# Attention outputs of both halves in one pool, and two of the second half's read-backs beside the last attention steps

## The chip, the cores and the metric

The kernel runs on one core of one Trainium2 chip. The metric is the device time of one execution in microseconds. Before the change the median of three runs is 1555.2 us (1551.68 to 1557.26). A separate, profiled execution gave the trace that is read here.

The engines are named as in the profile: PE (matrix products; PEld its weight loads), DVE (vector), ACT (scalar), POOL (GpSimd) and SP, which here only issues transfers. PE, DVE, ACT, POOL and SP each run their own list of instructions in order. Matrix products accumulate in PSUM; other tiles lie in SBUF, and "DRAM" names hold data that goes out to the chip's main memory and comes back.

## The reference

One layer of a streaming encoder on x of 1024 positions by 1024 channels, float32. Two attention branches (8 heads of 64 each) share one input projection; each is projected to 1024 channels, both are merged by sigmoid gates, and an output projection, a residual LayerNorm and a gated feed-forward part follow:

```python
proj = h @ w_in[l]
q_a, k_a, v_a, f_a, q_c, k_c, v_c, gate_a, gate_c = jnp.split(proj, split_points, axis=-1)
o_a = _forgetting_attention(heads_a(q_a), heads_a(k_a), heads_a(v_a), f_a + b_f[l])
o_c = _chunk_band_attention(heads_c(q_c), heads_c(k_c), heads_c(v_c), rel_bias[l])
merged = (jax.nn.sigmoid(gate_a) * (o_a @ w_br_fox[l])
          + jax.nn.sigmoid(gate_c) * (o_c @ w_br_chunk[l]))
mix = merged @ w_out[l]
x = _layer_norm(alpha * x + (1.0 + g1) * mix, ln1_g[l], ln1_b[l])
h = _layer_norm(x) * (1.0 + sc2) + sh2
u = _causal_depthwise_conv(h @ w_up[l], conv_w[l], conv_b[l])
a, val = jnp.split(u, 2, axis=-1)
y = (jax.nn.silu(a) * val) @ w_down[l]
x = _layer_norm(alpha * x + (1.0 + g2) * y, ln2_g[l], ln2_b[l])
```

## The kernel before, in words

**Precision.** A float32 product is made of three products of a rounded type: each operand is split into "hi" (a cast) and "lo" (what the cast left). Hence names in pairs: oh and ol, wh and wl, mh and ml; and each product comes as three matmuls, L192 to L194.

**Attention.** It works out unnormalised outputs, head by head, transposed, for two halves of 512 positions. They go to DRAM as od[half, i], 128 rows (two heads) by 512 positions each, i = 0 to 7. i = 4 to 7 is one branch, 0 to 3 the other. The reciprocals of the softmax sums go to rd, one row a head. Between attention steps PE is given pieces of other products (a "stream" of units); the last of these are the gates' pre-activations psg, whose sigmoid's core (ACT, L385) is stored to gd. Preparation of later weights (dr, td) runs on POOL up to about 648 us.

**Read-backs.** An attention output is used as a pair of i: ost<-od (512 KB), two transfers ort<-rd (256 KB each) that broadcast the reciprocals to the partitions of their head, a product (L794), the cast to oh on ACT (L797) and the subtraction to ol on DVE (L798). load_o, a generator, does one pair at each next(). For half 0 it goes through the pairs 4, 6, 2, 0: the first three are issued and multiplied on POOL, while the last attention steps run; the pair 0 is issued on SP and multiplied on DVE. For half 1 it goes through 4, 6, 2, 0, all on SP and DVE, one after each of the merge's first four branches. The transfers land in wop's tags wh and wl, two buffers each, so the third pair needs the buffers of the first.

**Merge.** branch(c, b, half) is a block of 128 channels c, a branch b and a half: 12 matmuls psb (L192 to L194), with branch weights brd and the four oh/ol of the half that belong to b (i = 4 to 7 for b = 1, 0 to 3 for b = 0). The accumulators come from mxp, 6 buffers. DVE multiplies psb with the gate sgl (L932), a tile of 512 KB loaded from gd for each (c, half); after b = 0 it adds the two (L935) and splits the result into m (ACT L940, DVE L941). The order is (0,1,0), (0,0,0), (1,1,0), (1,0,0), (0,1,1), (1,1,1), (0,0,1), (1,0,1), then c = 2 to 7, half by half. SP's list holds the weights, the gates and the read-backs one behind the other. The order within an engine is set by the program's text: an instruction stands where the code issues it, and buffers are given by pools in turn, which wait for the buffer's last reader.

**After it.** mixed is the output projection with w_out pieces (wod), residual and norms, then the up-projection's first heads. ready() loads and splits the first up-weights (sgl<-in_w_up on POOL).

**Pools.** o (half 0's outputs) and m1p are opened at the attention's end, o1 (half 1's) in the merge; after the merge o and o1 are closed, and w2 (w_out pieces 5 to 7) and mx (x rows, norm vectors, x2) are opened in their place.

Of the kernel before, what the change touches and what calls it, by code (L numbers as in the profile page):

```python
# [12 lines left out]
F32 = mybir.dt.float32  # L13
F32R = mybir.dt.float32r
AF = mybir.ActivationFunctionType
ALU = mybir.AluOpType
# [3 lines left out]
P = 128  # L20
S = 1024
D = 1024
NT = S // P
KD = D // P
H = 512
# [3 lines left out]
DH = 64  # L29
# [15 lines left out]
def body(ctx, tc, a, out):  # L45
# [38 lines left out]
    od = dram.tile([2, 8, P, H], F32, name="od", tag="od")  # L84
# [111 lines left out]
    def halves(half):  # L196
        return slice(half * H, (half + 1) * H)
# [583 lines left out]
    sy.dma_start(out=g1row, in_=rowd[0].partition_broadcast(P))  # L781
    m1_cm, m1p = opened(name="m1p", bufs=1, side="right")
    o_cm, op_ = opened(name="o", bufs=1, side="right")

    def load_o(half, os_, pairs, pool, tag, bufs, rpool, rtag, op_, early=0):
        for n, i in enumerate(pairs):
            dma, eng = (po, po) if n < early else (sy, ve)
            st = pool.tile([P, 2, H], F32, name=nm("ost"), tag=tag, bufs=bufs)
            dma.dma_start(out=st, in_=od[half, i : i + 2].rearrange("b p s -> p b s"))
            rt = rpool.tile([P, 2, H], F32, name=nm("ort"), tag=rtag, bufs=bufs)  # L790
            for h in range(2):
                row = rd.rearrange("(p h) s -> h p s", h=2)[h, i : i + 2, halves(half)]
                dma.dma_start(out=rt[h * DH : (h + 1) * DH], in_=row.partition_broadcast(DH))
            eng.tensor_tensor(out=st, in0=st, in1=rt, op=ALU.mult)  # L794
            hi = op_.tile([P, 2, H], F32R, name=nm("oh"), tag=f"oh{i}")
            lo = op_.tile([P, 2, H], F32R, name=nm("ol"), tag=f"ol{i}")
            se.copy(out=hi, in_=st)  # L797
            ve.tensor_sub(out=lo, in0=st, in1=hi)  # L798
            for b in range(2):
                os_[i + b] = (hi[:, b, :], lo[:, b, :])  # L800
# [103 lines left out]
    if True:  # L904
# [10 lines left out]

        def merge(os_, reading):
            ms = [[None] * KD for _ in range(2)]
# [129 lines left out]
        o1_cm.__exit__(None, None, None)  # L1047
        o_cm.__exit__(None, None, None)
# [3 lines left out]
        mx_cm, mx = opened(name="mx", bufs=1)  # L1052
        h_11, h_21 = [], []
# [3 lines left out]
        def rows(n):  # L1057
            for t in range(len(xs), n):
                xs.append(mx.tile([P, D], F32, name=nm("xr"), tag="xr", bufs=4))
                sy.dma_start(out=xs[t], in_=a["x"][t * P : (t + 1) * P, :])  # L1060

        rows(2)
        l1g = mx.tile([P, D], F32, name="l1g", tag="l1g", bufs=1)
        l1b = mx.tile([P, D], F32, name="l1b", tag="l1b", bufs=1)
        sy.dma_start(out=l1g, in_=a["ln1_g"].partition_broadcast(P))
# [4 lines left out]
        def begin(t):  # L1070
            x2s.append((mx if t < 4 else mxb).tile([P, D], F32, name=nm("x2"), tag="x2", bufs=4))
            for g in live:
                next(g, None)
            g = norms(t, xs[t], x2s[t], t < NT - 1)
            next(g)
            for old in live:
                next(old, None)
            live[:] = [g]

        turning = None  # L1080
        for group in ((0, 1), (2,), (3,), (4,), (5,), (6,), (7,)):
# [26 lines left out]

    mx_cm.__exit__(None, None, None)
    wo_cm.__exit__(None, None, None)  # L1110
    hd_cm.__exit__(None, None, None)
    w2_cm.__exit__(None, None, None)
    m1_cm.__exit__(None, None, None)
    x1 = x2s[4:]
    yp_cm, yp = opened(name="yp", bufs=3, side="right")
# [376 lines left out]
```

## Time and profile before

| | |
|---|---|
| median of three runs | 1555.2 us (1551.68 to 1557.26) |
| profiled execution | 1550.4 us, its span 1548.6 us |
| PE busy | 1500.3 us, 97% of the span, 7663 matmuls |
| DVE, ACT, POOL busy | 67%, 47%, 43% |
| DMA | 300.76 MB, 194 GB/s in the mean |
| last attention product | begins at 691.14 us |
| merge's first branch / first branch with c = 2 | 703.96 / 742.37 us |

Times within the span are microseconds from its start. A row of a time line has the start, the duration, the engine and line, the operation with its output and inputs, and in brackets how long the engine had been idle and what released it. An engine name with q (SPq, POOLq) is its issuing of transfers. In the chain of waits, a DMA row lasts from issue to landing. A matmul's own duration (0.39 us) is longer than its spacing, since matmuls are pipelined: the spacing of starts is what counts.

### The profile page before, as it was taken

What the parts mean: (1) busy time and instruction counts of PE and PEld (TensorE: products, weight loads), DVE (VectorE), ACT (ScalarE), POOL (GpSimd) and SP (SyncE); (2) the same over time, 40 slices, a digit from 0 to 9 for tenths busy, and PEclk for the clock granted to TensorE, in tenths of its full rate; (3) what the DMA queues carried; (4) which work ended last, traced back from release to release, by engine and by line L of the source; (5) the groups of instructions that cost most, each with busy time, mean ns of one, the idle gap of its engine ahead of it and who ended that gap; (6) DMA issues with size and microseconds to landing.
All of it is one profiled execution on the core that took longest, in us unless ns stands there. A gap on an engine that the chain in (4) does not pass through costs nothing.

```text
span 1548.6 us, 21684 instructions
## 1 busy us (share of the span) xinstructions
PE 1500.3 (97%) x7663; PEld 1264.7 (82%) x7663; DVE 1031.5 (67%) x2024; ACT 725.5 (47%) x1344; POOL 658.6 (43%) x607
## 2 busy tenths in 40 slices
PE   6999999999999999996999998999999999999996
PEld 3788898889888988885888887888888888888885
DVE  6756666566656565555446786777778776845798
ACT  3555555455444454442113565544544554555451
POOL 0039888887877877630000005454455453000000
PEclk9999999999999999998999999999999999999999
DMA  9157666766666579768764385443344323697552
GB/s 370 47 167 216 213 199 213 218 190 200 215 230 211 182 266 303 246 181 253 244 225 174 129 272 172 136 152 133 123 139 147 116 102 101 240 342 249 191 189 76
DMA packets 121053, 300.76 MB, mean 194 GB/s; under 512 B 12512, under 2 KB 21424, under 8 KB 120944
## 3 DMA queue, kind: packets, MB, share of 16 engines
q1 hardware_dynamic: 81504, 181.05, 35.4%
q0 software_dynamic: 25344, 92.02, 18.0%
q10 hardware_dynamic: 14096, 26.31, 4.8%
q8 instruction: 60, 0.98, 0.3%
q14 instruction: 49, 0.40, 0.1%
HBM read 206.69 MB, written 84.25 MB: 188 GB/s over the span
## 4 chain that ended last, share of the span: by engine, by line
PE 74%; POOL 9%; DMA 8%; DVE 5%; issue 2%; ACT 1%; SPq 0%; DVEq 0%; ACTq 0%; POOLq 0%
PE psu L861 24%; PE psd L1309 4%; PE psd L1310 4%; PE psd L1308 4%; PE pso L508 3%; PE psg L192 3%; PE psg L194 3%; PE psg L193 3%; DMA wod<-dr 3%; POOL dr L553 2%; PE pst L494 2%; POOL acc L559 2%; POOL dr L556 2%; DMA brd<-dr 2%; PE psm L957 2%
## 5 line engine op out<-in xcount | busy, mean ns | idle before, releaser
L861 PE MATMUL psu<-hc,wx 128*128 128x512 f32 x792 | 185.8, 389 | 2.4 <-ACT wx L849 2.0
L861 PEld LDWEIGHTS psu<-hc,wx 128*128 128x128 f32 x792 | 148.5, 188 | 34.0 <-ACT wx L849 2.7
L1157 DVE SCALAR_TENSOR_TENSOR pcv<-u,convp,pcv 128x1024 f32<-128x1024 f32 x88 | 113.2, 1286 | 45.4 <-ACT pcv L1155 44.4
L1298 DVE TENSOR_TENSOR op<-rw,op 128x512 fp32r<-128x512 f32 x146 | 93.3, 689 | 52.9 <-ACT op L1297 52.7
L1297 ACT CAST op<-rw 128x512 fp32r<-128x512 f32 x146 | 85.1, 623 | 87.0 <-PE psd L1310 41.7
L457 ACT ACTIVATE s<-s,mx 128x640 f32<-128x640 f32 (+7 forms) x128 | 94.7, 740 | 54.9 <-DVE mx L451 53.4
L1309 PE MATMUL psd<-op,op 128*128 128x512 f32 x292 | 113.6, 389 | 0.9 <-DVE op L1298 0.9
L1310 PE MATMUL psd<-op,op 128*128 128x512 f32 x292 | 113.6, 389 | 0.0
L1308 PE MATMUL psd<-op,op 128*128 128x512 f32 x292 | 113.1, 389 | 0.0
L497 ACT CAST pt<-pst 128x512 fp32r<-128x512 f32 (+1 forms) x192 | 82.2, 451 | 63.1 <-PE pst L494 61.7
L498 DVE TENSOR_TENSOR pt<-pst,pt 128x512 fp32r<-128x512 f32 (+1 forms) x192 | 96.1, 519 | 17.4 <-ACT pt L497 15.5
L192 PE MATMUL psq<-h1h,wh 128*128 128x512 f32 x256 | 103.8, 407 | 1.7 <-DVE h1h L188 1.3
L192 PE MATMUL psg<-h1h,wh 128*128 128x512 f32 x256 | 103.7, 405 | 0.0
L194 PE MATMUL psq<-h1h,wl 128*128 128x512 f32 x256 | 100.9, 394 | 0.9 <-DVE wl L112 0.9
L193 PE MATMUL psq<-h1l,wh 128*128 128x512 f32 x256 | 100.7, 393 | 0.0
L194 PE MATMUL psg<-h1h,wl 128*128 128x512 f32 x256 | 100.3, 392 | 0.0
L193 PE MATMUL psg<-h1l,wh 128*128 128x512 f32 x256 | 100.2, 391 | 0.0
L556 POOL TENSOR_SCALAR dr<-dr,cond 128x512 f32<-128x512 f32 x56 | 90.9, 1625 | 8.3 <-DMA dr<-in_w_ada 7.3
L508 PE MATMUL pso<-pt,vs 128*128 128x256 f32 x608 | 90.4, 288 | 0.8 <-DVE pt L498 0.8
L508 PEld LDWEIGHTS pso<-pt,vs 128*128 128x128 f32 x608 | 81.3, 191 | 7.9 <-ACT pt L497 3.0
L112 DVE TENSOR_TENSOR wl<-ws,wh 128x1024 fp32r<-128x1024 f32 x38 | 61.1, 1609 | 39.1 <-ACT wh L111 39.1
L494 PE MATMUL pst<-ident,s 128*128 128x128 f32 x528 | 83.1, 273 | 0.8 <-DVE pt L498 0.7
(299 smaller groups left out, 3926.8 us busy)
## 6 DMA issues: line engine op xcount, KB each, us to landing
ws<-in_w_up SPq DMA_DIRECT2D x34, 512.0 KB, 3.8
dr<-in_w_ada POOLq DMA_DIRECT2D x32, 512.0 KB, 4.5
dr<-in_w_down POOLq DMA_DIRECT2D x22, 512.0 KB, 5.1
td<-dr POOLq DMA_DIRECT2D x22, 512.0 KB, 4.8
rw<-td SPq DMA_DIRECT2D x44, 256.0 KB, 4.5
yd<-y SPq DMA_DIRECT2D x20, 512.0 KB, 2.8
rw<-yd SPq DMA_DIRECT2D x40, 256.0 KB, 4.7
rw<-sd SPq DMA_DIRECT2D x33, 256.0 KB, 4.8
```

Of the source, the lines that this page charges most:

```text
L192: pe.matmul(ps, wh, xh, start=start, stop=False)
L193: pe.matmul(ps, wh, xl, start=False, stop=False)
L194: pe.matmul(ps, wl, xh, start=False, stop=stop)
L494: pe.transpose(ps[:, b * P : (b + 1) * P], st[:, c0 : c0 + P], ident)
L498: ve.tensor_sub(out=dl, in0=src, in1=dh)
L508: pe.matmul(ps[:, 0:256], vs[:, h % 2, j0 + j, :], pt[j // 4][:, c, j % 4, :], start=j == 0 and c == 0, stop=j == nj - 1 and c == 1)
L556: po.tensor_scalar_mul(x[:, k % 2, :] if k else acc, x[:, k % 2, :], cond[:, k : k + 1])
L861: pe.matmul(ps, w[:, a_, k, :], h[k][b_], start=first, stop=k == 3 and a_ == 1, skip_group_check=on)
L1157: ve.scalar_tensor_tensor(out=ps, in0=u[b][:, 2 - d : S + 2 - d], scalar=cp[:, 2 - d : 3 - d], in1=ps, op0=ALU.mult, op1=ALU.add)
L1308: pe.matmul(ps[t], g[:, 0, ts], d[:, 0], start=start, stop=False, skip_group_check=on)
L1309: pe.matmul(ps[t], g[:, 0, ts], d[:, 1], start=False, stop=False, skip_group_check=on)
L1310: pe.matmul(ps[t], g[:, 1, ts], d[:, 0], start=False, stop=stop, skip_group_check=on)
```

## The change

Both halves' outputs get one pool o of 16 tiles, opened at the attention's end; m1p is opened later, where o1 was. load_o becomes read_o, a generator with two steps (issue the transfers; multiply and split). Five pairs are read on POOL beside the last attention steps: those of half 0 as before, in tiles of the qs and m1 tags, and the pairs 4 and 6 of half 1 in tiles of the attention's v values (tag vs), one wide tile of which holds a pair's outputs and its reciprocals. The pair 0 of half 0 stays with SP and DVE. The last two pairs of half 1 are issued on SP ahead of the merge's gate loads, into the two buffers of wop, and multiplied after the second and the fourth branch. After the merge, the pool o isn't closed: its tiles are used again, by tag, for the w_out pieces 5 to 7, the x rows, the norm vectors and the first four x2. ready() takes its load buffer from the pool hd.

```diff
-    def load_o(half, os_, pairs, pool, tag, bufs, rpool, rtag, op_, early=0):
...
-            yield
-
-    o0, o1 = {}, {}
-    reading = load_o(0, o0, (4, 6, 2, 0), ap0, "qs", 4, ap0, "m1", op_, 3)
-    for _ in range(3):
-        next(reading)
+    def read_o(half, i, st, rt, early=False):
+        dma, eng = (po, po) if early else (sy, ve)
+        dma.dma_start(out=st, in_=od[half, i : i + 2].rearrange("b p s -> p b s"))
+        for h in range(2):
+            row = rd.rearrange("(p h) s -> h p s", h=2)[h, i : i + 2, halves(half)]
+            dma.dma_start(out=rt[h * DH : (h + 1) * DH], in_=row.partition_broadcast(DH))
+        yield
+        eng.tensor_tensor(out=st, in0=st, in1=rt, op=ALU.mult)
+        hi = op_.tile([P, 2, H], F32R, name=nm("oh"), tag=f"oh{half}{i}")
+        lo = op_.tile([P, 2, H], F32R, name=nm("ol"), tag=f"ol{half}{i}")
+        se.copy(out=hi, in_=st)
+        ve.tensor_sub(out=lo, in0=st, in1=hi)
+        for b in range(2):
+            os_[half][i + b] = (hi[:, b, :], lo[:, b, :])
+        yield
+
+    def wide_of():
+        x = ap0.tile([P, 2, NT, P], F32, name=nm("ost"), tag="vs", bufs=3)
+        return [x[:, j].rearrange("p (b a) c -> p b (a c)", b=2) for j in range(2)]
+
+    os_ = {}, {}
+    reading = []
+    for half, i in ((0, 4), (0, 6), (1, 4), (1, 6), (0, 2)):
+        reading.append(read_o(half, i, *(wide_of() if half else pair_of(ap0, ("qs", "m1"), 4)), True))
+        next(reading[-1])
+    for r in reading:
+        next(r)
     stream.finish(len(stream.units))
     begun()
-    next(reading)
+    for _ in read_o(0, 0, *pair_of(ap0, ("qs", "m1"), 4)):
+        pass
...
-    o1_cm, o1p = opened(name="o1", bufs=1, side="right")
+    m1_cm, m1p = opened(name="m1p", bufs=1, side="right")
...
                 branch(*unit)
-                if n < 4:
-                    next(reading)
+                if n in (1, 3):
+                    for _ in reading.pop(0):
+                        pass
...
-        ms = merge((o0, o1), load_o(1, o1, (4, 6, 2, 0), wop, "wh", 2, wop, "wl", o1p))
+        reading = [read_o(1, i, *pair_of(wop, ("wh", "wl"), 2)) for i in (2, 0)]
+        for r in reading:
+            next(r)
+        ms = merge(reading)
...
-        w2_cm, w2p = opened(name="w2", bufs=3, side="right")
-        ws += [parted_w(wod[k], w2p) for k in range(5, KD)]
+        for tags in (("oh04", "ol04"), ("oh06", "ol06"), ("oh02", "ol02")):
+            ws.append([again(tag, True) for tag in tags])
+            for x, j in zip(ws[-1], (2, 0)):
+                sy.dma_start(out=x.bitcast(F32), in_=wod[len(ws) - 1, j : j + 2].rearrange("j p n -> p j n"))
...
-                    ready(c, hdp, mx)
+                    ready(c, hdp, hdp)
```

POOL's list at the attention's end, before: the last preparation steps (dr, td), then three pairs of half 0 (4, 6, 2), then the first up-weights.

```order
L588 TENSOR_TENSOR dr_6658<-dr_6658 128x512
L595 DMA td<-dr_6658 128x2x512
L789 DMA ost_7787<-od 128x2x512
L793 DMA ort_7789<-rd 64x2x512 x2
L794 TENSOR_TENSOR ost_7787<-ost_7787,ort_7789 128x1024
L793 DMA ort_7799<-rd 64x2x512 x2
L793 DMA ort_7809<-rd 64x2x512
L789 DMA ost_7797<-od 128x2x512
L793 DMA ort_7809<-rd 64x2x512
L794 TENSOR_TENSOR ost_7797<-ost_7797,ort_7799 128x1024
L789 DMA ost_7807<-od 128x2x512
L794 TENSOR_TENSOR ost_7807<-ost_7807,ort_7809 128x1024
```

And now, from the second product on (the first, of the pair 4 of half 1, stands ahead of these; its load from od stands before the last dr step). ost_7784 is half 0's pair 4, ost_7789 its pair 6, ost_7798 half 1's pair 6, ost_7802 half 0's pair 2.

```order
L786 DMA ost_7784<-od 128x2x512
L789 DMA ost_7785<-rd 64x2x512 x2
L791 TENSOR_TENSOR ost_7784<-ost_7784,ost_7785 128x1024
L789 DMA ost_7790<-rd 64x2x512 x2
L789 DMA ost_7803<-rd 64x2x512
L786 DMA ost_7789<-od 128x2x512
L789 DMA ost_7803<-rd 64x2x512
L791 TENSOR_TENSOR ost_7789<-ost_7789,ost_7790 128x1024
L786 DMA ost_7798<-od 128x2x512
L789 DMA ost_7798<-rd 64x2x512 x2
L791 TENSOR_TENSOR ost_7798<-ost_7798 128x1024
L786 DMA ost_7802<-od 128x2x512
```

Three products in a row have become five, and two pairs of half 1 have come among those of half 0; the reciprocals of half 0's pair 2 are still asked for early.

SP's list at the merge's start, before and then now (wh and wl from brd are branch weights, sgl the gates; the first pair after them is half 1's 4 before, and its 2 now):

```order
L913 DMA wh_7969<-brd 128x2x512
L913 DMA wl_7970<-brd 128x2x512
L926 DMA sgl_7914<-gd 128x2x512
L789 DMA ost_7930<-od 128x2x512
L793 DMA ort_7932<-rd 64x2x512 x2
L789 DMA ost_7959<-od 128x2x512
L793 DMA ort_7961<-rd 64x2x512 x2
L926 DMA sgl_7973<-gd 128x2x512
L789 DMA ost_7989<-od 128x2x512
L793 DMA ort_7991<-rd 64x2x512 x2
```

```order
L921 DMA wh_7979<-brd 128x2x512
L921 DMA wl_7980<-brd 128x2x512
L786 DMA ost_7925<-od 128x2x512
L789 DMA ost_7926<-rd 64x2x512 x2
L786 DMA ost_7927<-od 128x2x512
L789 DMA ost_7928<-rd 64x2x512 x2
L934 DMA sgl_7939<-gd 128x2x512
L934 DMA sgl_7983<-gd 128x2x512
```

Four pairs have become two, and the first gate load has moved behind them.

DVE's list there now (before, an L932 pair and its sum stood ahead of the first product of half 1):

```order
L795 TENSOR_TENSOR ol_7829<-ost_7802,oh_7828 128x1024
L795 TENSOR_TENSOR ol_7895<-ost_7888,oh_7894 128x1024
L791 TENSOR_TENSOR ost_7925<-ost_7925,ost_7926 128x1024
L795 TENSOR_TENSOR ol_7976<-ost_7925,oh_7975 128x1024
L791 TENSOR_TENSOR ost_7927<-ost_7927,ost_7928 128x1024
L940 SCALAR_TENSOR_TENSOR sgl_7939<-sgl_7939,psb_7941 128x512
L940 SCALAR_TENSOR_TENSOR sgl_7939<-sgl_7939,psb_7955 128x512
L795 TENSOR_TENSOR ol_8020<-ost_7927,oh_8019 128x1024
L943 TENSOR_TENSOR sgl_7939<-sgl_7939 128x512
```

The two products of half 1 that are left (ost_7925 its pair 2, ost_7927 its pair 0) now stand ahead of the first gate products L940 (L932 before), and the subtraction of the pair 0 behind two of these.

More of the change, by code (lines that the diff above doesn't have):

```diff
@@ L781, in body @@
     sy.dma_start(out=g1row, in_=rowd[0].partition_broadcast(P))
-    m1_cm, m1p = opened(name="m1p", bufs=1, side="right")
     o_cm, op_ = opened(name="o", bufs=1, side="right")
-    def load_o(half, os_, pairs, pool, tag, bufs, rpool, rtag, op_, early=0):
[L786 to L800, printed above, removed]
-            yield
@@ new lines, in pair_of @@
+    def pair_of(pool, tags, bufs):
+        return [pool.tile([P, 2, H], F32, name=nm("ost"), tag=t, bufs=bufs) for t in tags]
+    def wide_of():
[6 more added lines that the diff above has]
+        next(reading[-1])
@@ L914, in parted_w, with merge @@
             return parts
-        def merge(os_, reading):
+        def merge(reading):
             ms = [[None] * KD for _ in range(2)]
@@ L1058, in rows @@
             for t in range(len(xs), n):
-                xs.append(mx.tile([P, D], F32, name=nm("xr"), tag="xr", bufs=4))
+                xs.append(again(("oh00", "ol00", "oh14", "ol14")[t % 4]))
                 sy.dma_start(out=xs[t], in_=a["x"][t * P : (t + 1) * P, :])
         rows(2)
-        l1g = mx.tile([P, D], F32, name="l1g", tag="l1g", bufs=1)
-        l1b = mx.tile([P, D], F32, name="l1b", tag="l1b", bufs=1)
+        l1g, l1b = again("oh16"), again("ol16")
         sy.dma_start(out=l1g, in_=a["ln1_g"].partition_broadcast(P))
@@ L1070, in begin @@
         def begin(t):
-            x2s.append((mx if t < 4 else mxb).tile([P, D], F32, name=nm("x2"), tag="x2", bufs=4))
+            x2s.append(again(("oh12", "ol12", "oh10", "ol10")[t]) if t < 4 else
+                       mxb.tile([P, D], F32, name=nm("x2"), tag="x2", bufs=4))
             for g in live:
@@ L1107, in body @@
             head(c)
-    mx_cm.__exit__(None, None, None)
     wo_cm.__exit__(None, None, None)
     hd_cm.__exit__(None, None, None)
-    w2_cm.__exit__(None, None, None)
     m1_cm.__exit__(None, None, None)
+    o_cm.__exit__(None, None, None)
     x1 = x2s[4:]
```

5 lines of the change are left out of this document (2 added, 3 removed).

## The prediction

> **What bounds the kernel now.** I read the page first, then a table of windows over the end of the attention and the merge, then who TensorE (PE) waits for, then the chain of waits through the stage, then the time lines of the engines and queues in it.
>
> The page, and the windows of the stages:
>
> ```profile
> span 1548.6 us, 21684 instructions
> PE 1500.3 (97%) x7663; PEld 1264.7 (82%) x7663; DVE 1031.5 (67%) x2024; ACT 725.5 (47%) x1344; POOL 658.6 (43%) x607
> ```
>
> ```profile
> 680.00:690.00 10.00, 10.00 (x61) 8.50 (x61) 5.81 (x10) 3.87 (x8) 0.21 (x1) 1.00 0.44 145
> 690.00:703.00 13.00, 13.00 (x66) 11.10 (x65) 5.59 (x6) 5.35 (x7) 0.00 (x0) 1.00 0.54 190
> 703.00:742.00 39.00, 27.37 (x100) 20.55 (x100) 17.47 (x20) 6.51 (x8) 0.00 (x0) 0.82 0.86 254
> 742.00:790.00 48.00, 48.00 (x214) 39.74 (x213) 24.76 (x37) 5.74 (x10) 0.00 (x0) 1.00 0.73 246
> ```
>
> The columns are the window, its length, the busy time (instructions) of PE, PEld, DVE, ACT and POOL, the granted clock, the DMA engines' share and GB/s. PE is the bound nearly everywhere; one stretch stands out. From 703 to 742 it is busy 27.37 of 39 us, at a clock of 0.82, while DMA is at 0.86. Before and after it PE is full. Of the 48.3 us that PE idles in the whole span, this stretch holds 11.6. POOL does nothing from 690 to 790, and DMA is half idle from 680 to 703. Who PE waits for, from 690 to 810:
>
> ```profile
> PE psb L192 <- ACT oh L797: 10.7, 2, 7.4
> PE psb L193 <- DVE ol L798: 0.9, 2, 0.5
> ```
>
> So all of it is the merge's first matmuls waiting for the attention outputs of the second half, "hi" (cast on ACT, L797) and "lo" (subtracted on DVE, L798). PE's time line, and then the chain of waits, there:
>
> ```profile
> 703.96 0.39 PE L192 MATMUL psb<-oh,wh 128*128 128x512 f32 x1
> 714.61 0.39 PE L194 MATMUL psb<-oh,wl 128*128 128x512 f32 x1
> 718.33 0.77 PE L192 MATMUL psb<-oh,wh 128*128 128x512 f32 x2 [3.33 <-ACT oh L797]
> 719.59 0.79 PE L193 MATMUL psb<-ol,wh 128*128 128x512 f32 x1 [0.49 <-DVE ol L798]
> 724.25 0.50 PE L193 MATMUL psb<-ol,wh 128*128 128x512 f32 x1 [0.39 <-DVE ol L798]
> 734.20 1.22 PE L192 MATMUL psb<-oh,wh 128*128 128x512 f32 x2 [7.38 <-ACT oh L797]
> 742.37 0.39 PE L192 MATMUL psb<-oh,ws 128*128 128x512 f32 x1
> ```
>
> ```profile
> 704.16 0.61 ACT sg L385
> 704.79 5.70 DMA gd<-sg
> 710.50 0.57 SPq L793
> 711.24 10.34 DMA sgl<-gd
> 721.76 1.28 DVE sgl L932 x2
> 723.04 1.16 DVE ol L798
> ...
> 725.33 6.39 DMA ort<-rd
> ...
> 733.11 1.05 ACT oh L797
> ...
> 736.26 0.43 PE psb L194
> ```
>
> The four branches of half 0 run without a wait from 703.96 to 714.61: 47 steps in 10.65 us, 0.2266 us a matmul. The first eight branches have 96 matmuls, 21.75 us at that pace. They took 742.37 - 703.96 = 38.41, so **16.66 us are lost**: 3.33 + 0.49 + 0.39 + 7.38 = 11.59 in waits, and 5.07 in slow matmuls after them (0.43 each at 736.26). The four pairs of half 1 are loaded through two buffers, so the third pair's product must wait until the first pair is split, and its load starts only then.
>
> **The change, part by part.** I write half/pair.
>
> *Two read-backs go from SP and DVE, in the merge, to POOL, before it.* The rows that price POOL's steps, and the queues that meet them:
>
> ```profile
> 648.47 0.73 POOL L789 DMA_DIRECT2D ost<-od  x1
> 657.52 3.09 POOL L794 TENSOR_TENSOR ost<-ost,ort 128x1024 f32<-128x1024 f32 x1 [6.16 <-DMA ort<-rd]
> 660.92 1.82 POOL L793 DMA_DIRECT2D ort<-rd  x3 [0.31 <-POOL ost L794]
> 670.11 2.39 POOL L794 TENSOR_TENSOR ost<-ost,ort 128x1024 f32<-128x1024 f32 x1 [6.00 <-DMA ost<-od]
> 672.43 0.75 POOL L789 DMA_DIRECT2D ost<-od  x1
> 676.87 3.34 POOL L794 TENSOR_TENSOR ost<-ost,ort 128x1024 f32<-128x1024 f32 x1 [3.69 <-DMA ost<-od]
> ...
> 682.98 1.31 SPq L793 DMA_DIRECT2D ort<-rd  x2
> ...
> 691.14 1.12 PE L508 MATMUL pso<-pt,vs 128*128 128x256 f32 x8
> ```
>
> A step costs POOL 12.1 us (648.47 to 660.61), 11.6 (660.92 to 672.50), and 7.8 where its reciprocal rows were asked for a step early (672.43 to 680.21). Now there are five, in the order 1/4, 0/4, 0/6, 1/6, 0/2, the first begun about a microsecond sooner because its first load stands ahead of two of POOL's last stores. By these rows they end at about 660, 671, 683, 695 and 702; with the later loads in the stretch where DMA is only 0.44 to 0.54 busy, I take **701** for the fifth. What waits for it: ACT's casts stand in order, the fifth ahead of the last two gate activations. The last of these ran at 704.16, and ahead of it the fifth cast (1.05), another activation (0.61) and the cast of 0/0 (1.05) must fit, so the fifth product may end at 701.4 without cost. Beyond that, each microsecond delays the gates' store by one. The cover is thin but there.
>
> The third product meets SP: the reciprocal load of 0/0 was issued at 682.98 and reuses a buffer that POOL's third product now frees, at about 683. DVE's product of 0/0 stands ahead of the last probability splits, on which PE's last eight value matmuls at 691.14 hang. Cost by the rows: nothing; about a microsecond later it would reach PE one for one.
>
> The Trainium skill, "SBUF — State Buffer", section "Who interferes with whom", says that a DVE instruction with two SBUF inputs contends with a GpSimd instruction that reads SBUF. By it, two more POOL products could hold DVE up for as long as they last, at most 2 x 3.34 = 6.7 us, and the forecast would lose what of that reached PE. The trace agrees that POOL's products vary from 2.39 to 3.34 us, but shows no PE wait beside the three that it has, so I put nothing into the sum for it.
>
> *What PE then runs without a wait.* The first six branches use 0/all and 1/4, 1/6 only: 72 x 0.2266 = 16.3 us, from 703.96 to **720.3**. The waits of 3.33, 0.49 and 0.39 go. The last two branches, (0,0,1) and (1,0,1), need 1/0.
>
> *The two read-backs that stay* (1/2, 1/0) are issued ahead of the gate loads:
>
> ```profile
> 704.90 0.41 SPq L926 DMA_DIRECT2D sgl<-gd  x1
> 708.26 2.82 SPq L793 DMA_DIRECT2D ort<-rd  x2
> 711.97 1.29 DVE L932 SCALAR_TENSOR_TENSOR sgl<-sgl,psb 128x512 f32<-128x512 f32 x2 [10.24 <-DMA sgl<-gd]
> 715.98 1.22 DVE L794 TENSOR_TENSOR ost<-ost,ort 128x1024 f32<-128x1024 f32 x1 [0.61 <-DMA ort<-rd]
> 720.62 1.23 DVE L794 TENSOR_TENSOR ost<-ost,ort 128x1024 f32<-128x1024 f32 x1 [1.08 <-DMA ort<-rd]
> ```
>
> Before, the first two pairs on SP landed at 715.98 and 720.62, with one gate load (512 KB) ahead; the second pair's last piece could not be issued until 710.50, when the gates' store had landed. Now that gate load is gone, a first up-weight load of 512 KB comes in on POOL's queue instead, and the last piece waits for branch weights only. I take 0.9 us off: the product of 1/0 at 719.7.
>
> *The gate loads slip.* SP's first now stands behind these and waits for the last gates' store, which landed at 710.49. It lands 7.1 us (704.90 to 711.97) to 10.3 us (the second one, 711.24 on) after issue: 717.6 to 720.8. With two pairs and the branch weights ahead of it, as that second one had, I take 720.8. PE has six accumulators for branches, so the seventh branch needs the first freed by DVE's L932, which needs that gate. DVE's order is product of 1/0, two L932, then the lo of 1/0, just as it was at 720.62, 721.76 and 723.04; then PE's third matmul came at 724.25. 0.9 us earlier: **723.3**.
>
> *The end of the first eight branches.* Two matmuls of the seventh run ahead; 22 x 0.2266 = 5.0 more give 728.3. PE idles some 2.5 us at 720.3. Will the clock fall? Windows of 2 us:
>
> ```profile
> 716.00:718.00 2.00, 0.00 (x0) 0.00 (x0) 1.20 (x1) 0.77 (x1) 0.00 (x0) 1.00 1.07 247
> 718.00:720.00 2.00, 1.17 (x3) 0.70 (x4) 1.23 (x1) 0.28 (x1) 0.00 (x0) 0.72 1.05 246
> 720.00:722.00 2.00, 2.00 (x6) 1.52 (x6) 1.38 (x2) 0.12 (x1) 0.00 (x0) 0.50 0.74 232
> ```
>
> After the gap of 3.33 us the clock was 0.72 and 0.50 for 4 us: 0.28 x 2 + 0.50 x 2 = 1.6 us lost. After 0.39 us nothing is seen. 2.5 is nearer to 3.33, so I charge 1.6: **729.9**, where it was 742.37. The Trainium skill, "TensorE: Matmul & The Clock Gate", section "What's actually happening", says the clock falls after an idle window of about 3.4 us. By it the shorter gap would cost no clock; the trace's 3.33 us gap lies at its edge and did cost it. By the rule the sum would be 1.6 us better.
>
> *The rest.* The wider pool takes over the buffers of later w_out pieces, x rows and norm vectors; their loads keep their places and the releases they wait for come no later, and PE is full from 742 to 790. DMA has room: over 703 to 790 it worked 39 x 0.86 + 48 x 0.73 = 69 of 87 us, and less of that work is left for 74.5. I charge 0.
>
> **Sum**: 742.4 - 729.9 = **12.5 us** less. The profiled execution, 1550.4 us around a span of 1548.6, becomes 1537.9. It lies 4.8 us under the median of the runs shown; on the median's scale 1555.2 - 12.5 = **1542.7 us**.
>
> **The rivals.**
>
> *A. POOL's queue is a little late, or the loads in the merge are.* POOL's fifth product at 703.2 (all steps at 11.6 and 7.8, no help from the quieter DMA) puts the gates' store, the gate load and the seventh branch 1.8 us back; DMA at 1.05 to 1.07 in the merge may hold the gates to 723 as well. Gain 8 to 11: 1544 to 1547. For it: little slack at 701.4. Against: landing is the larger part of a step (6.00 and 6.16 us of idle), and should be shorter where DMA is half idle.
>
> *B. The loads come sooner.* The gate at 717.6 and 1/0 with it: hardly a stall, no lost clock. Gain up to 16.6: 1538.6. Against it: DMA at 1.05 to 1.07 from 716 to 720, so nothing lands faster.
>
> *C. POOL's third product is really late (the loss).* If a step takes much longer with more loads at once, the load of 0/0 waits for it on SP, DVE stands with that product ahead of the last probability splits, and PE stops at 691 with everything behind. Price one for one beyond 684; the gain is eaten when the third product ends at about 696.5 instead of 683, three steps of 16 us, and beyond that the kernel is slower: at 18 us a step, by some 5 us, 1560. For it: two pairs more share POOL and the DMA engines there. Against: no step so far took over 12.1.
>
> *D. The merge starts its later branches earlier, and waits for weights or gates there instead.* The branches of c = 2 and 3 run 12 us sooner, on loads that SP issues behind the same queue. Against: those 69 us of DMA work, less two pairs (1 MB each, 4 us at 254 GB/s), still fit into 74.5; the gain is lost only if the loads keep their old times. Time: 1553 to 1556.
>
> **How the numbers follow.** Forecast 0.5, A 0.25, B 0.08, C 0.07 (0.05 of it a loss), D 0.1. The forecast's own range is 1541 to 1545. Timed runs of this kernel differ by 5.6 us, so I allow 2 us below B and for a part of D above A: 1537 to 1552. 0.3%, 4.7 us, is about what a measurement of this kernel can tell from no change. Faster by more: forecast, A, B and a small part of C and D, 0.86; same 0.08; slower 0.06.
>
> **What would show it.** Right: POOL's five products from 656 to 701; no PE wait up to 720; one wait of 2 to 3 us at the seventh branch, on ACT's cast or DVE's lo of 1/0 or L932; the first matmul with c = 2 near 730; the end of the merge 12 us sooner and the span with it. Wrong: waits at 691 (C), at 707 to 715, several microseconds at 720 (A), waits between 730 and 800 (D), or equal stage times with gaps downstream.

## The result, and the profile after

The changed kernel takes 1546.82 us in the median of 12 runs (1540.68 to 1549.31), the kernel before 1553.85 (12 runs, 1550.63 to 1562.56). The ratio is **0.995, interval 0.9932 to 0.9968**: about 7.0 us faster by the medians, clear of the 0.3% that was taken for no change, and some way short of the 12.5 forecast. In two later sets, beside other runs of the kernel before, the ratio was 0.992 (0.9895 to 0.9945) and 0.9946 (0.9927 to 0.9965), by the medians some 9.4 and 9.0 us.

The first trace of the changed kernel is of its fastest run, 1540.7 us around a span of 1538.9. Its windows of the stages, with the columns as before:

```profile
680.00:690.00 10.00, 10.00 (x57) 8.29 (x57) 5.97 (x13) 4.25 (x9) 4.29 (x4) 1.00 0.93 296
690.00:703.00 13.00, 11.76 (x64) 9.88 (x63) 4.90 (x5) 5.13 (x8) 5.48 (x3) 1.00 0.80 258
703.00:742.00 39.00, 37.47 (x163) 30.18 (x162) 24.38 (x31) 8.97 (x12) 0.59 (x1) 1.00 0.83 281
742.00:790.00 48.00, 48.00 (x213) 39.77 (x212) 23.21 (x35) 5.59 (x9) 0.00 (x0) 1.00 0.65 221
```

From 703 to 742 PE is now busy 37.47 of 39 us at full clock, where it had 27.37 at 0.82. But something new stands ahead of it: from 690 to 703 PE has lost 1.24 us, and from 680 to 690 the DMA engines are 0.93 busy, where they were 0.44. Who PE waits for, from 640 to 810:

```profile
PE pso L508 <- DVE pt L498: 1.2, 1, 1.2
PE psb L194 <- DMA wl<-brd: 1.2, 1, 1.2
PE psb L193 <- DVE ol L795: 0.3, 1, 0.3
```

The two long waits for the second half's outputs are gone, and only 0.3 us of waiting for it is left. The two waits of 1.2 us are new: for the last probability splits of the attention (L498), and for branch weights. PE's time line:

```profile
696.08 2.06 PE L508 MATMUL pso<-pt,vs 128*128 128x256 f32 x15 [1.24 <-DVE pt L498]
...
716.26 0.50 PE L194 MATMUL psb<-oh,wl 128*128 128x512 f32 x1 [1.18 <-DMA wl<-brd]
...
727.80 0.50 PE L193 MATMUL psb<-ol,wh 128*128 128x512 f32 x1 [0.35 <-DVE ol L795]
...
732.95 0.39 PE L192 MATMUL psb<-oh,ws 128*128 128x512 f32 x1
```

The first branch with c = 2 begins at 732.95, not 742.37. The merge's first branch, though, began at 708.89 (before: 703.96). So the first eight branches took 24.1 us instead of 38.4, 14.3 less, and 4.9 us were lost before them.

**How much of that is chance.** The same gate activation (ACT, L385), in a part of the program that the change doesn't touch, starts in the two traces at

```profile
580.30 0.60 ACT L385 ACTIVATE sg<-psg 128x512 f32<-128x512 f32 x1 [1.39 <-PE psg L194]
```

```profile
582.38 0.60 ACT L385 ACTIVATE sg<-psg 128x512 f32<-128x512 f32 x1 [2.32 <-PE psg L194]
```

The first row is of the kernel before, the second of the changed one: 2.1 of the 4.9 us were there before anything had changed. In all 14 traces of this study the activation lies between 578.4 and 583.5. The times from it on are therefore what is compared below: from it to the merge's first branch (A), from there to the merge's last matmul (M), and from that to the end of the span (R), worked out from the rows of each trace in the same way.

| trace | A | M | R |
|---|---|---|---|
| before | 123.7 | 103.5 | 741.2 |
| changed, first trace | 126.5 | 89.1 | 740.9 |
| changed, second (e1) | 133.9 | 90.0 | 740.9 |
| changed, third (e11) | 129.3 | 91.5 | 741.4 |

M is 12.0 to 14.4 us shorter, and R is the same within 0.3. What differs from run to run is A: 2.8, 10.2 and 5.6 us longer than before. Means: M 13.3 us gained, A 6.2 lost, 7.1 left. The timed medians differ by 7.0, 9.4 and 9.0 us in the three sets; means of three traces against a single one of before can't be held to more than that.

### The profile page after: what moved, and what is told of

Its sections match the earlier page's. It is cut to its first block, busy times and chain, and to the rows that moved or that the text cites. A ratio compares the mean times of both kernels' runs of the same rounds, so it can differ in the third digit from the quotient of the medians.

```text
span 1538.9 us, 21695 instructions
## 1 busy us (share of the span) xinstructions
PE 1499.2 (97%) x7663; PEld 1263.4 (82%) x7663; DVE 1032.2 (67%) x2022; ACT 723.9 (47%) x1344; POOL 665.0 (43%) x615
## 4 chain that ended last, share of the span: by engine, by line
PE 85%; DVE 6%; DMA 4%; POOL 2%; issue 1%; ACT 1%; DVEq 0%; ACTq 0%; POOLq 0%; SPq 0%
PE psu L869 25%; PE pso L508 4%; PE psd L1323 4%; PE psd L1324 4%; PE psd L1322 4%; PE psg L192 3%; PE psg L193 3%; PE psg L194 3%; PE pst L494 3%; PE psq L194 3%; PE psq L193 3%; PE psq L192 3%; PE psv L295 2%; PE psv L294 2%; PE psv L296 2%; PE pss L442 2%
## 5 line engine op out<-in xcount | busy, mean ns | idle before, releaser
L498 DVE TENSOR_TENSOR pt<-pst,pt 128x512 fp32r<-128x512 f32 (+1 forms) x192 | 96.0, 518 | 17.7 <-ACT pt L497 15.9
L112 DVE TENSOR_TENSOR wl<-ws,wh 128x1024 fp32r<-128x1024 f32 x38 | 63.5, 1671 | 39.2 <-ACT wh L111 39.2
```

The lines of the kernel that those rows point to most:

```text
L498: ve.tensor_sub(out=dl, in0=src, in1=dh)
```

## The experiments

The question was then what makes the attention's end late, and by so different amounts. Theory A: the two added read-backs crowd it. Rivals: the pool, the added products, or chance. M, A and R of all the kernels are in the table at the end of this section.

**e1, the changed kernel again.**

> The changed kernel once more, for a second trace. In the first trace the merge's first branch began at 709.1 us (before: 704.0) and the branches with c = 0 and 1 took 23.9 us (before: 38.4). Theory A (the two added read-backs crowd the transfers at the attention's end, and the merge starts about 3 us late for it, the other 2 us being chance): merge start 706 to 710. Rival C (all 5 us were chance): merge start 703 to 706. Where the timed runs of the changed kernel lie 6 us above the first trace, something of 3 to 6 us must show here that the first trace did not have, a lower clock after a wait being the candidate. Ratio 0.995.

Median of the timed runs 1544.3 us; the traced run took 1549.6. The merge began at 716.8, later than any theory had it. SP's and DVE's time lines and, last, POOL's, in this trace:

```profile
687.76 0.32 SPq L470 DMA_DIRECT2D rd<-rt  x1
694.20 1.31 SPq L789 DMA_DIRECT2D ost<-rd  x2
...
681.41 3.05 DVE L112 TENSOR_TENSOR wl<-ws,wh 128x1024 fp32r<-128x1024 f32 x1
...
686.78 0.95 DVE L469 RECIPROCAL rt<-psr 32x128 f32<-32x128 f32 x1 [1.65 <-PE psr L464]
...
699.63 1.23 DVE L791 TENSOR_TENSOR ost<-ost,ost 128x1024 f32<-128x1024 f32 x1 [7.23 <-issue]
700.77 1.28 DVE L498 TENSOR_TENSOR pt<-pst,pt 128x512 fp32r<-128x512 f32 x2
...
680.99 2.39 POOL L791 TENSOR_TENSOR ost<-ost,ost 128x1024 f32<-128x1024 f32 x1 [7.55 <-DMA ost<-od]
683.32 0.75 POOL L786 DMA_DIRECT2D ost<-od  x1
684.07 1.21 POOL L789 DMA_DIRECT2D ost<-rd  x2
```

and its waits of PE:

```profile
PE pso L508 <- DVE pt L498: 3.7, 1, 3.7
PE psr L464 <- ACT s L457: 1.6, 1, 1.6
PE psb L192 <- ACT oh L794: 1.6, 1, 1.6
PE psb L193 <- DVE ol L795: 0.6, 1, 0.6
```

They tell the chain. The reciprocals of the last heads are stored by a small transfer, rd<-rt (16 KB), and read back for the first half's pair 0. SP issues the read-back only when the store has landed: 6.44 us later here, against 1.68 before (681.30 to 682.98). DVE's product of pair 0 waits for the read-back (7.23 us idle, start at 699.63), the last two splits L498 stand behind it, and PE's last value matmuls wait 3.66 us for them.

Here POOL has issued 1 MB for pair 6 of the second half shortly ahead of the store (683.32 to 685.28). In the first trace it did so only from 684.41 to 686.37, with the store issued at 684.74, so that can't be the whole of it. Directly ahead of the store in SP's list stands a weight load of 512 KB, ws<-brd. Its issue, and the row with the time to landing, in the kernel before, in the first trace and in e1:

```profile
677.97 0.36 SPq L913 DMA_DIRECT2D ws<-brd  x1
ws<-brd SPq DMA_DIRECT2D x1, 512.0 KB, 4.7
682.70 0.49 SPq L921 DMA_DIRECT2D ws<-brd  x1
ws<-brd SPq DMA_DIRECT2D x1, 512.0 KB, 4.6
684.49 0.36 SPq L921 DMA_DIRECT2D ws<-brd  x1
ws<-brd SPq DMA_DIRECT2D x1, 512.0 KB, 9.2
```

It lands at about 682.7, 687.3 and 693.7, and the read-back of the reciprocals is issued 0.3 to 0.5 us later (682.98, 687.62, 694.20). In e1 this load was slow. In the first trace it took as long as before, but was issued 2.04 us ahead of the store instead of 3.33: pair 0's load, which stands ahead of it, waited for the attention outputs od<-o (256 KB), and these took 6.5 us to land instead of 2.0. POOL issued 1.5 MB around them (673.35 to 676.50), where it had issued 0.5 MB before (672.43).

The clock falls too:

```profile
700.00:710.00 10.00, 8.49 (x33) 7.53 (x34) 4.50 (x6) 3.46 (x5) 2.36 (x1) 0.66 0.64 230
```

(PEclk is 0.66 in this window of the same trace. PE resumed at 701.51; from 701.5 to 707.5 the granted clock was 0.53, so some 2.8 us more were lost, 6 x 0.47.) A second thing comes on top: DVE's subtraction L112 took 3.05 us beside POOL's third product. Before, in its place, it took

```profile
676.73 1.22 DVE L112 TENSOR_TENSOR wl<-ws,wh 128x1024 fp32r<-128x1024 f32 x1
```

and POOL's product, which came second then, took 3.34 instead of 2.39. Whichever of the two comes first, the other waits. Here it cost PE the 1.6 us at L464.

**e2, the pool alone.** All four pairs of the second half read in the merge, as before:

```diff
-    for half, i in ((0, 4), (0, 6), (1, 4), (1, 6), (0, 2)):
+    for half, i in ((0, 4), (0, 6), (0, 2)):
...
-                if n in (1, 3):
-                    for _ in reading.pop(0):
+                if n < 4:
+                    for _ in next(reading)():
                         pass
...
-        reading = [read_o(1, i, *pair_of(wop, ("wh", "wl"), 2)) for i in (2, 0)]
-        for r in reading:
-            next(r)
+        reading = iter([lambda i=i: read_o(1, i, *pair_of(wop, ("wh", "wl"), 2)) for i in (4, 6, 2, 0)])
```

> One part alone: the one pool for both halves' outputs, its tiles used again after the merge, and the earlier buffer of the first up-weights, but no pair of the second half read early: its four pairs are read in the merge by SP and DVE through two buffers, one after each of the first four branches. Theory A: same as before within 2 us (1552 to 1556), the merge's first branch at 703 to 706 and the branches with c = 0 and 1 in 37 to 40 us. Rival B (the pool itself makes the attention's end late): first branch at 707 or later, 3 to 5 us slower than before.

1552.55 us, ratio 0.9993 (0.9978 to 1.0009); A 123.7, M 103.4. The pool costs and brings nothing; it only makes room.

**e3, one early pair.** As e2, with (1, 4) in the early list and (6, 2, 0) in the merge.

> Only pair 4 of the second half is read early on POOL; its pairs 6, 2 and 0 are read in the merge through the two buffers. Theory A: the start of the merge is 1 to 2 us later than before instead of 5; PE waits at the fifth branch for pair 6 (some 2 us) and at the seventh for pair 0, the third through two buffers (4 to 6 us); gain about 5 to 7 us over the kernel before. If the two pairs share their gain evenly and cost nothing early: 7 to 8 us. If waiting for the third buffer is all that matters: 1 to 3 us.

1550.64 us, ratio 0.9971 (0.9959 to 0.9983): some 3 us, less than expected. A is 124.2, so one early pair costs the attention's end almost nothing (0.5); the store of the reciprocals took 1.53 us (SP 683.15 to 684.68). But M is 98.1, for PE's time line still shows the third load through two buffers:

```profile
720.03 0.73 PE L192 MATMUL psb<-oh,wh 128*128 128x512 f32 x2 [1.17 <-ACT oh L794]
731.33 1.22 PE L192 MATMUL psb<-oh,wh 128*128 128x512 f32 x2 [7.48 <-ACT oh L794]
```

The long wait, 7.38 us before, stays at 7.48; it is gone where no third pair is left for the two buffers, in the changed kernel, which also issues its two pairs sooner, ahead of the gate loads. The gain is not shared evenly between the pairs: M falls by 5.4 us with the first and by 6.6 to 9.0 more with the second.

**e4, the two early read-backs left out**, the first half's tiles used in their place:

```diff
-    for half, i in ((0, 4), (0, 6), (1, 4), (1, 6), (0, 2)):
+    for half, i in ((0, 4), (0, 6), (0, 2)):
...
+        os_[1].update({i: os_[0][i] for i in range(4, 8)})
+        for tag in ("oh14", "ol14", "oh16", "ol16"):
+            ve.memset(op_.tile([P, 2, H], F32, name=nm("z"), tag=tag), 0.0)
```

> Leaves out the two early read-backs of the second half: the merge's branches use the first half's pairs 4 and 6 in their place, so neither their transfers nor their products, casts and subtractions are made. What the early reading costs at the attention's end is then the difference to the changed kernel. Theory A: merge's first branch at 703.5 to 706, 3 us or more sooner than with the reads; total 1540 to 1543, 3 to 6 us under the changed kernel. Rival C: first branch as late as with them, total within 2 us of the changed kernel.

1545.22 us, ratio 0.9935 (0.9916 to 0.9955): not under the changed kernel's median beside it (1544.3), so the total that theory A expected, 1540 to 1543, did not come. A did what it said: 124.4, no wait at the last value matmuls. But the merge, beginning sooner, waits longer for what is left: PE stood 4.1 us for the second half's pair 0 (M 95.6). What the attention's end gives up, the merge partly takes back, since the read-back of pair 0 and the gates set the seventh branch.

**e5, pair 0's product on POOL**, so that DVE's last splits no longer stand behind it:

```diff
-        dma, eng = (po, po) if early else (sy, ve)
+        dma, eng = (po, po) if early else (sy, po if (half, i) == (0, 0) else ve)
```

> The changed kernel, but the product of the first half's pair 0 made on POOL instead of DVE (its loads stay on SP). In the two traces of the changed kernel PE waited 1.2 and 3.7 us for the last probability splits, which stand on DVE behind this product. If that order is what makes the attention's end late (theory A, by way of DVE's queue): no wait of PE at the last value matmuls, merge start 704 to 708, and 2 to 5 us less than the changed kernel (1540 to 1543). If POOL's sixth product merely moves the lateness to the casts and the gates' store: no wait there, but one of 2 to 4 us in the merge, and the same total within 2 us.

1541.16 us, ratio 0.9912 (0.989 to 0.9934). PE's waits in its trace, from 640 to 810:

```profile
PE psb L193 <- DVE ol L795: 1.9, 2, 1.3
PE psb L192 <- ACT oh L794: 1.3, 1, 1.3
```

No wait is left at the last value matmuls, and A is 123.6, as before the change, although the small store still took 3.62 us. The lateness went by way of DVE's queue. Some of it came back as a wait of 1.26 us at the second branch, for the lo of pair 0.

**e6, the transfers without the products.**

```diff
-        eng.tensor_tensor(out=st, in0=st, in1=rt, op=ALU.mult)
+        if not (early and half):
+            eng.tensor_tensor(out=st, in0=st, in1=rt, op=ALU.mult)
```

> Leaves out the normalising products of the second half's pairs 4 and 6 on POOL, and keeps all their transfers. It tells the transfers from the products. If the transfers cause the late end of the attention (the small store of the reciprocals took 6.3 and 2.9 us in the changed kernel's traces, 1.7 before): PE still waits 1 us or more at the last value matmuls and the merge starts at 707 or later. If the products do it, by holding up DVE's subtractions with two inputs in SBUF (one took 3.05 us beside a product, 1.22 alone): no wait there, store of the reciprocals under 2 us, start 704 to 706.5, total 2 to 4 us under the changed kernel.

1541.99 us, ratio 0.9915 (0.9891 to 0.994). Its trace, SP's time line and PE's waits:

```profile
682.76 0.32 SPq L470 DMA_DIRECT2D rd<-rt  x1
687.90 1.31 SPq L789 DMA_DIRECT2D ost<-rd  x2
```

```profile
PE pso L508 <- DVE pt L498: 2.1, 1, 2.1
...
```

Without the products the store still takes 5.14 us, PE still waits 2.1 us, and A is 127.8. So the transfers are enough, in a kernel in which POOL issues them sooner (its last load at 677.72, in the first trace of the changed kernel at 694.29). The median is 2 to 5 us under the changed kernel's three medians, so the products may add a part, as the 3.05 us in e1 show that they can; how much in the mean, these few runs don't settle.

**e7, pair 6's loads issued by SP** as soon as their data are there, its product on POOL:

```diff
-        dma, eng = (po, po) if early else (sy, ve)
+        dma = po if early and (half, i) != (1, 6) else sy
+        eng = po if early else ve
```

> The changed kernel, with the loads of the second half's pair 6 issued on SP as soon as their data are there, instead of on POOL behind its third product; the product stays on POOL. That takes 1 MB of transfers out of the time when the reciprocals of the last heads are stored and read back. If these transfers are the cause: store of the reciprocals under 2 us, no wait at the last value matmuls, merge start 704 to 707, 2 to 5 us less than the changed kernel. If not: the wait stays, total within 2 us. What can go wrong: SP's weight loads for the gates stand behind these loads; if the data are later than SP, PE waits for weights before 680.

1546.55 us, ratio 0.9937 (0.9912 to 0.9962), no better. In its trace SP issued pair 6's loads at 625.00 and 627.36, POOL issued no load between 677.2 and 688.0, and the store, issued at 684.39, still took 3.30 us. So the store is late without the 1 MB of pair 6 near it. The rows of SP's list fit here too: od<-o took 5.0 us to land, the weight load 6.3 (at about 687.4), and the read-back was issued 0.3 us later. DVE's product of pair 0 then took 2.53 us beside POOL's last one, and PE waited 5.1 us (A 132.9).

**e8, the first eight branches on the blocks 0 and 2**, whose weights are there early:

```diff
-            order_ = [(0, 1, 0), (0, 0, 0), (1, 1, 0), (1, 0, 0), (0, 1, 1), (1, 1, 1), (0, 0, 1), (1, 0, 1)]
-            order_ += [(c, b, half) for c in range(2, KD) for half in range(2) for b in (1, 0)]
+            order_ = [(0, 1, 0), (0, 0, 0), (2, 1, 0), (2, 0, 0), (0, 1, 1), (2, 1, 1), (0, 0, 1), (2, 0, 1)]
+            order_ += [(c, b, half) for c in (1, 3, 4, 5, 6, 7) for half in range(2) for b in (1, 0)]
+            for c in range(3):
+                held[c] = [x.rearrange("p j (k n) -> p (j k) n", k=4) for x in parted_w(brd[c])]
```

> The changed kernel, with the merge's first eight branches on the channel blocks 0 and 2 instead of 0 and 1: block 2's weights land at 690, block 1's only after the last gate matmul. It takes away the wait for weights in the first trace of the changed kernel (1.2 us at 716). 0 to 1.5 us less than the changed kernel (1544 to 1546); the start of the merge as with it. If the loads that then come later (block 1 for the ninth branch) are late instead: a wait at 730 to 735 and no gain.

1542.47 us, ratio 0.9918 (0.9897 to 0.994), below the 1544 to 1546 expected. The wait for weights is gone, M is 89.2 as in the first trace, and the wait at the last value matmuls stays (1.7 us). Since neither the second nor the third trace of the changed kernel waits for these weights, this is at most a part of the 1.4 to 4.4 us by which the median is lower, and four runs don't show it apart from A's scatter.

**e9, e5 and e8 together.**

> The changed kernel with the product of pair 0 on POOL and the first eight branches on the blocks 0 and 2: what the two took away alone were different waits (PE at the last value matmuls; the weights of block 1), so if both are causes of their own, the gains add: 2 us under the better of them, 1538 to 1540. What stays: the second branch waits 1 to 1.5 us for the lo of pair 0, since POOL multiplies it last. If both only cured the same chance lateness: 1541 to 1543.

1540.82 us, ratio 0.9931 (0.9906 to 0.9955): by the ratio no better than e5 alone, so the two gains did not add. In e5's trace PE did not wait for the weights either. A 125.0, M 90.7.

**e10 and e12, the kernel of e9 with branch 1 of both halves and blocks first; e11, the changed kernel beside e12.**

```diff
-            order_ = [(0, 1, 0), (0, 0, 0), (2, 1, 0), (2, 0, 0), (0, 1, 1), (2, 1, 1), (0, 0, 1), (2, 0, 1)]
+            order_ = [(c, b, half) for b in (1, 0) for half in range(2) for c in (0, 2)]
```

> As the last, and the first eight branches go through branch 1 of both halves and blocks first (pairs 4 and 6 alone), branch 0 after: the pair 0 of the first half is then needed 10.9 us after the merge's start instead of 2.7. No wait at the second branch; PE waits only at the seventh, for pair 0 of the second half, 1 to 2 us. 1 to 1.5 us under the last one: 1537 to 1539. If the accumulators are then freed too late (a gate load serves branch 1 now, branch 0 only later): a wait of 1 to 3 us at the seventh and eighth, and no gain over it.

> The changed kernel a third time, on the same chip and in the same rounds as the next. By the two traces so far it has an end of the attention that is late by a different amount each time (a wait of 1.2 or 3.7 us at the last value matmuls, and once a lower clock after it). Theory A: again a wait of 1 to 5 us there, on DVE's last probability splits behind the product of pair 0; median 1543 to 1548. If the wait does not come back, it was chance.

> The kernel with pair 0's product on POOL and branch 1 first, beside the changed kernel. Theory A: no wait over 0.5 us at the last value matmuls, a wait of 2 to 3.7 us at the seventh branch, median 1538 to 1541, 4 to 7 us under the changed kernel. If the two medians lie within 2 us, the cures were chance.

e10: 1539.45 us, ratio 0.9921 (0.9897 to 0.9945). e11, the changed kernel: 1543.82, ratio 0.9946 (0.9927 to 0.9965). e12: 1541.06, ratio 0.9929 (0.9912 to 0.9946); that is 2.8 us under e11, less than the 4 to 7 expected. PE's waits in e11 and then in e12:

```profile
PE pso L508 <- DVE pt L498: 3.2, 1, 3.2
PE psb L192 <- ACT oh L794: 2.0, 1, 2.0
PE psb L193 <- DVE ol L795: 0.6, 1, 0.6
```

```profile
PE psb L192 <- ACT oh L794: 3.1, 1, 3.1
PE psb L193 <- DVE ol L795: 0.2, 1, 0.2
```

The wait at the last value matmuls is there in each of the three traces of the changed kernel (1.2, 3.7, 3.2 us), and in none of the four that have the product on POOL (e9's wait of 1.2 us for L498 falls at 646.83, at earlier value matmuls). The wait that remains, 3.1 us at the seventh branch in e10 and e12, is for pair 0 of the second half; 1 to 2 us had been expected in e10.

| trace | early pairs of half 1 | pair 0's product | store rd<-rt, us | A | M | R |
|---|---|---|---|---|---|---|
| before | none | DVE | 1.68 | 123.7 | 103.5 | 741.2 |
| e2 | none | DVE | 1.52 | 123.7 | 103.4 | 742.2 |
| e4 | none (left out) | DVE | 1.73 | 124.4 | 95.6 | 742.2 |
| e3 | one | DVE | 1.53 | 124.2 | 98.1 | 742.0 |
| changed | two | DVE | 2.88 | 126.5 | 89.1 | 740.9 |
| e1 | two | DVE | 6.44 | 133.9 | 90.0 | 740.9 |
| e11 | two | DVE | 3.38 | 129.3 | 91.5 | 741.4 |
| e6 | two, no product | DVE | 5.14 | 127.8 | 92.8 | 740.9 |
| e7 | two, one by SP | DVE | 3.30 | 132.9 | 92.9 | 740.7 |
| e8 | two | DVE | 3.24 | 125.8 | 89.2 | 740.9 |
| e5 | two | POOL | 3.62 | 123.6 | 92.5 | 741.1 |
| e9 | two | POOL | 5.98 | 125.0 | 90.7 | 741.6 |
| e10 | two | POOL | 3.19 | 124.4 | 92.7 | 740.9 |
| e12 | two | POOL | 3.76 | 123.9 | 93.6 | 740.9 |

The store's time is from the issue of rd<-rt to that of the read-back which waits for it. It is 1.5 to 1.7 us in every kernel with at most one early pair, 2.9 or more in every kernel with two. A is late only where, besides, the product stands on DVE (2.1 to 10.2 us over before); with it on POOL A is within 1.3 us of before.

Two more times follow the same line. The attention outputs od<-o that pair 0's load waits for landed 2.0 to 2.1 us after issue in the four traces with at most one early pair, after 5.0 to 7.6 us in nine with two, and after 2.7 in e6. And in 12 of the 14 traces the read-back of the reciprocals is issued 0.3 to 0.6 us after the landing of the weight load that stands ahead of the store in SP's list (1.0 in e5, 3.6 in e9). That the store is late for its place behind that load is read from these times; no run put it on another queue.

**A version that is likely faster still.** Pair 0's product on POOL and branch 1 first (e10, e12) had medians of 1539.45 and 1541.06 us, against 1546.82, 1544.3 and 1543.82 for the changed kernel, and 1551.38 and 1552.77 for the kernel before in the same sets as these. Over the 12 and the 25 runs, from different chips, the medians are 1540.8 and 1544.9. In the one set where they stood side by side (e11, e12), the two ratios to the kernel before have intervals that overlap: that it beats the kernel before is shown, that it beats the changed one is likely.

## Why the prediction was right or wrong

The direction and the range were right (1537 to 1552, measured 1546.8), the size was not: 7.0 us where 12.5 were forecast (9.4 and 9.0 in the later sets). The time fell just above the range of the forecast's own case (1541 to 1545) and into that of rival A (1544 to 1547), though not for A's reasons.

**The merge**, forecast at 12.5 us less: M is 14.4, 13.5 and 12.0 us less in the three traces. The terms, from the merge's start: six branches without a wait held, but for 1.18 us of waiting for block 1's weights in the first trace, which no term had priced. The gate was put 10.3 us after its issue; it landed after some 9.2 (716.01 to 725.20; 9.8 and 10.2 in e1 and e11), and its issue did follow the landing of the last gates' store. The third matmul of the seventh branch was put 19.3 us after the start (723.3 - 703.96); it came after 18.9, 19.9 and 19.8. The 1.6 us for a slow clock came in one trace of three: in the first PE stood 0.35 us there and the clock stayed at 1.00; in e1 it stood 1.57 and 0.64 us, and the clock stayed at 1.00 too; in e11 it stood 1.96 and 0.64 us, and a stretch of 3.4 us at half clock followed, 1.7 us lost.

**"Cost by the rows: nothing"**, of the attention's end, is the step that failed: A grew by 2.8, 10.2 and 5.6 us. Of this the wait at the last value matmuls, with the slow clock after it, is 1.2, 6.5 and 4.7 us. The rest (some 1.4, 3.8 and 0.9) had been lost before the last reciprocals were ready, in e1 1.6 of it by L112's collision; a wait of 1.75 us there at 599.51, and one of 0.50 in the first trace at 629.37, fell ahead of any read-back and are chance. The place was named rightly, the load of pair 0's reciprocals, DVE's product behind it, and behind that the splits on which the last value matmuls hang; also that it reaches PE one for one. The price was read from the wrong wait. The prediction watched POOL's third product, estimated for 683 (it ended at 683.4 in e1 and 684.5 in the first trace), and priced a loss only from its end at 684 on (rival C). What was late was the other thing that the same load waits for, the landing of the 16 KB store rd<-rt, behind SP's own weight load, and with it the load itself. The transfers there were priced at a DMA share of 0.44, that of the trace of before, when the change itself puts 1 MB into just that stretch: 0.93 in the trace after. The two added pairs also push half 0's read-backs, 1.5 MB, into the stretch where od<-o is stored. e6 shows it without the products, e3 that one pair leaves room enough, e5 that the path to PE is DVE's order.

**Rival C** had this mechanism's place and the wrong trigger, and its chance of 0.07 was far too low for a loss that all three traces show in part. **Rival A**, POOL's fifth product late, was answered by the trace: it ended at 702.6 instead of 701, and the last gates' store was still issued 0.6 us after its activation began. **Rival D** fell: R is 740.9 to 741.4 against 741.2, so nothing of the gain was lost downstream. **Rival B** came in part, in the first trace's merge: hardly a stall (0.35 us), no lost clock, and M 14.4 us shorter where 12.5 had been summed.

**The Trainium skill's rule** on two SBUF inputs ("SBUF — State Buffer", "Who interferes with whom") was put at nothing, on the ground that three products had cost no wait. The second trace agrees with the rule: 3.05 us for a DVE subtraction beside a POOL product, 1.22 alone, and 1.6 us of it reached PE. In the first trace none did. It depends on whether product and subtraction meet. That they meet more often with two more products is not shown: before, two of POOL's three products were stretched (3.09 and 3.34 us against 2.39), in the first trace none of the five. The rule on the clock gate ("TensorE: Matmul & The Clock Gate", "What's actually happening") would have taken the 1.6 us out of the sum; half-clock stretches after gaps of 1.96 and 0.64 us (e11) speak against reading its 3.4 us as a limit below which a gap is free.

## What to carry to other kernels

When loads are moved to an earlier stretch, price that stretch with the moved bytes in it and with what they push back, and look first at the small transfers on its dependent path and at what stands ahead of them in their own queue: a 16 KB store that took 1.5 to 1.7 us with at most one early pair took 2.9 to 6.4 with two. An instruction that waits for such a transfer should not stand in an engine's queue ahead of work that the bound engine needs; moving one product to another engine's queue brought the attention's end back to what it was. A bottleneck of two buffers goes when the last load that has to reuse them goes: one early pair shortened that stage by 5.4 us and left its longest wait, both shortened it by 12.0 to 14.4.

## What the runs showed of the hardware that was not expected

The same instructions, up to 580 us, took between 578.4 and 583.5 us in 14 traces, and between 579.0 and 582.9 in the four of the set of e1 to e4; why was not followed. A single trace doesn't tell a few microseconds of a change from that. DVE's subtraction of two SBUF operands and POOL's product of two exclude one another nearly whole: 1.22 and 2.39 us alone, 3.05 us for the one or 3.34 for the other when they met. And the granted clock fell after short waits in some runs only: after 3.66 us in e1, 3.19 in e11 and 2.14 in e6, and after two waits close together in e11 (1.96 and 0.64 us) and e5 (1.28 and 0.63; 0.50 from 728 to 730), but not after 1.80 and 0.64 us in e9, nor in the first trace, whose longest was 1.24.
